# Two chunks of both up steps without the seven-product scheme, bias sums on another engine, and a new layout of the down step's tiles

## The chip, the cores and the metric

The kernel runs on one core of one Trainium2 chip, as one launch. The metric is the device time of a run in microseconds, the median of several runs. Engines are named as in the profile: PE (TensorE, matrix products), DVE (VectorE), ACT (ScalarE), POOL (GpSimd), SP (SyncE, which here mostly issues transfers).

## The reference, cut to what matters

Two transformer blocks in fp32, over 1024 tokens of width 1024. The parts that the change touches are the two feed-forwards, the biases of the second block's neighbourhood attention, and the norm at the start of the second block:

```python
# end of block 1, then the norm that ends it
u = rmsnorm(h, norm_mlp_g) @ w_up            # 1024 -> 4096
h = h + jnp.square(jax.nn.relu(u)) @ w_down  # 4096 -> 1024
x = rmsnorm(h, norm_final_g)
# block 2
h = rms_norm(x, ln1_g);  z = h @ w_in + b_in
...
bias = rpb[:, d_row[:, None, None, :, None], d_col[None, :, :, None, :]]
scores = jnp.where(valid[:, :, None, :], scores + bias[None], -1e30)
...
h2 = rms_norm(x, ln2_g)
x = x + jnp.square(jax.nn.relu(h2 @ w_ff1)) @ w_ff2
return rms_norm(x, lnf_g)
```

## The kernel before, in words

Every fp32 product is computed in three: each operand is split into a high part (the value rounded to the fast format, a copy on ACT, L130) and a low part (the rest, a subtraction on DVE or POOL, L131), and high by high, high by low and low by high are summed in PSUM. In the trace these two lines are those of all splits; which one a row belongs to is told by its tile: `w` are weights, `x` the normed tokens of an up step, `part` the operands of a down step.

A feed-forward is `ff_up`, then `ff_down`. It runs twice: after block 1's cross attention, and at the very end. `ff_up` goes over 16 chunks c of 256 hidden columns. In each chunk the product of tokens (two halves j of 512) and weights (two halves k of the 1024 inputs by two halves f of the chunk) is done as seven products of sums of quarter blocks in place of eight products of the blocks themselves: product i takes X[i], a sum of the quarter blocks of the tokens, and W[c][i], one of the weights. A product is 12 matmuls 128x128 by 128x512 (L967), so a chunk has 84. Products 1 and 2 take tokens of the first half alone (X1, X2, split in a block ahead of the loop), all others take sums with the second half. `second()` makes those: it norms the second half (`normed`, tiles xn, L903), transposes it on PE (L242, into tp and sc), forms t1 and t2 on DVE (L938, L939) and splits X5, X6, X7, X3 and X4. It stands behind four products of chunks 0 and 1. In chunks 0 and 1 the products come in pairs, (0,1), (1,1), (0,2), (1,2), (0,5), and so on; from chunk 2 on the order is (c,1), (c-1,4), (c,5), (c,6), (c,2), (c,3), (c,7). Product 1 is copied from PSUM by ACT (L973), 5, 6 and the results by DVE (L852), the squared relu is L981 on ACT with a DVE product, or L985 on DVE. Results, tiles t2k out of 12 buffers, are stored to DRAM (`hid_d`) by transfers that POOL issues (L987), four a chunk.

In the first `ff_up` there is side work: `bias_tables`. A table is written to DRAM (`rpb_d`), and in 12 steps of two 128x2x384 tiles (`bt`, two slots) it is loaded (L1219), the mask tile is added (L1225, POOL, two 128x384 per tile), and four stores put it to `bias_d` (L1226). All of its transfers are issued by POOL, in the same queue as the hidden values' stores. A step (`work[0]`) comes behind product 4 and the loads of the next (`work[1]`) behind product 3.

`ff_down` reads the hidden values back and does seven products of 16 steps, each step 12 matmuls by four PSUM banks (L1128). Its tiles are laid, by `layout("down")`, over those of the up step: `wpool` (left parts), `xpool` (streamed operands), `rpool` (right parts) and nine kept tiles. Where a pool lies on a tile of the up step, its first writer waits until that tile has been read: over a t2k tile that is the landing of its store, over a weight tile the last matmul that reads it.

`block2` starts with the last down product's sums, row tile by row tile (`finish`, L1284 the product with the norm's gain, L1299 and L1302 two squares on ACT with row sums), then xn (L1313), then `to_T`, the transposes. A scheduler sets the final order on every engine by priorities, `high_priority` and `issue_after`; each engine then runs its instructions in that order, and a waiting one holds those behind it.

## Time and profile before

| | us |
|---|---|
| median of three runs | 3135.36 (3133.58 to 3139.14) |
| the profiled execution | 3136.28 |
| its span | 3134.5 |
| PE busy in it | 2913.7 (93%) |
| DVE busy | 2203.8 (70%) |
| ACT busy | 1233.1 (39%) |
| POOL busy | 420.1 (13%) |

Terms and rows are read from the profiled execution. Times in rows of a timeline count from the start of its span. The first up step runs from 857.85 to about 1219.9, the first down step until 1535.4, block 2 begins there, the second up step at 2451.12 and the second down step at 2806.63.

### The profile page before, as it was taken

The numbers are of one execution on the slowest core, as the hardware profiler recorded it, in microseconds if no ns is written. First come the engines' busy times: TensorE is split into PE (matmuls) and PEld (weight loads), VectorE is DVE, ScalarE is ACT, GpSimd is POOL, SyncE is SP. The second block draws the span as 40 slices with busy tenths as digits, with TensorE's granted clock in tenths as the row PEclk, the third lists the DMA queues.
The fourth block names the chain that finished last, engine by engine and source line by source line (L and its number), as shares of the span: only waits on it lengthen the run. The fifth ranks groups of instructions, "written<-read, shape, count | busy, mean of one in ns | idle before, by whom it ended". The sixth has DMA issues, their size and how long they took to land.

```text
span 3134.5 us, 39994 instructions
## 1 busy us (share of the span) xinstructions
PE 2913.7 (93%) x14548; PEld 2441.5 (78%) x14548; DVE 2203.8 (70%) x3895; ACT 1233.1 (39%) x2276; POOL 420.1 (13%) x450
## 2 busy tenths in 40 slices
PE   7898899999969989999689999999999699989997
PEld 5798888788858867788567789898788588877786
DVE  6997777555677875997557787644345776749976
ACT  4122665332432222444456655444211522224444
POOL 3240110000002661000101222200000011100000
PEclk9998999999989999999889999999999899999999
DMA  3225573211114667652211323567842233356522
GB/s 123 63 86 167 181 216 93 67 48 61 68 65 156 202 211 285 221 169 78 89 58 60 125 86 107 172 194 235 281 129 74 74 112 114 108 207 246 195 88 81
DMA packets 252501, 422.86 MB, mean 135 GB/s; under 512 B 27893, under 2 KB 130832, under 8 KB 252304
## 3 DMA queue, kind: packets, MB, share of 16 engines
q1 hardware_dynamic: 214240, 305.86, 30.5%
q0 software_dynamic: 28832, 95.57, 8.9%
q10 hardware_dynamic: 9232, 18.88, 1.6%
q8 instruction: 115, 1.88, 0.2%
q14 instruction: 82, 0.67, 0.1%
HBM read 310.75 MB, written 111.69 MB: 135 GB/s over the span
## 4 chain that ended last, share of the span: by engine, by line
PE 62%; DVE 14%; issue 9%; DMA 7%; POOL 3%; ACT 3%; SPq 1%; DVEq 0%; ACTq 0%; POOLq 0%
PE mm L208 16%; PE fd L1128 14%; PE ff L967 8%; PE mm L179 5%; PE mm L180 5%; PE mm L181 5%; DVE acc L423 2%; PE pv L669 2%; PE tp L735 1%; PE pv L1589 1%; DMA bt<-rpb_d 1%; DVE keep L1015 1%; PE tp L242 1%; DVE part L131 1%; POOL w L131 1%
## 5 line engine op out<-in xcount | busy, mean ns | idle before, releaser
L967 PE MATMUL ff<-x,w 128*128 128x512 f32 x2688 | 632.9, 396 | 52.3 <-DVE w L131 23.3
L967 PEld LDWEIGHTS ff<-x,w 128*128 128x128 f32 x2688 | 511.2, 191 | 169.0 <-DVE w L131 24.1
L1128 PE MATMUL fd<-part,part 128*128 128x512 f32 x2688 | 622.9, 393 | 13.1 <-ACT part L130 9.3
L1128 PEld LDWEIGHTS fd<-part,part 128*128 128x128 f32 x2688 | 505.5, 189 | 130.4 <-DVE part L131 14.9
L208 PE MATMUL mm<-xh,w 128*128 128x512 f32 x1792 | 532.4, 394 | 0.5 <-ACT lruC L1461 0.3
L208 PEld LDWEIGHTS mm<-xh,w 128*128 128x128 f32 x1792 | 337.1, 189 | 69.2 <-ACT lruC L1461 1.6
L130 ACT ACTIVATE part<-keep 128x512 fp32r<-128x512 f32 x384 | 224.4, 624 | 288.1 <-PE fd L1128 265.7
L208 PE MATMUL mm<-xl,w 128*128 128x512 f32 x896 | 316.6, 393 | 0.0
L131 DVE TENSOR_TENSOR part<-keep,part 128x512 fp32r<-128x512 f32 x384 | 249.9, 682 | 52.4 <-ACT part L130 52.1
L130 ACT ACTIVATE w<-raw 128x1024 fp32r<-128x1024 f32 (+1 forms) x132 | 134.9, 1033 | 287.7 <-PE mm L180 115.7
L131 POOL TENSOR_TENSOR w<-raw,w 128x1024 fp32r<-128x1024 f32 x56 | 169.9, 3039 | 548.1 <-ACT w L130 523.2
L208 PEld LDWEIGHTS mm<-xl,w 128*128 128x128 f32 x896 | 169.3, 189 | 33.5
L852 DVE TENSOR_TENSOR t2k<-ff,t2k 128x512 f32<-128x512 f32 x160 | 109.7, 688 | 105.0 <-PE ff L967 94.3
L423 DVE SCALAR_TENSOR_TENSOR acc<-u,conv_wh,acc 128x1023 f32<-128x1023 f32 (+14 forms) x120 | 172.8, 1480 | 3.1 <-ACT acc L418 1.3
L234 DVE TENSOR_TENSOR h<-h,mm 128x512 f32<-128x512 f32 x176 | 119.5, 685 | 78.4 <-PE mm L181 77.7
L179 PE MATMUL mm<-w,xh 128*128 128x256 f32 x512 | 147.3, 288 | 15.3 <-DVE u L449 11.5
L130 ACT ACTIVATE w<-wr 128x512 fp32r<-128x512 f32 x160 | 97.4, 630 | 151.9 <-PE ff L967 62.3
L180 PE MATMUL mm<-w,xh 128*128 128x256 f32 x512 | 146.4, 286 | 0.0
L181 PE MATMUL mm<-w,xl 128*128 128x256 f32 x512 | 146.4, 286 | 0.0
L987 POOL DMA_DIRECT2D hid_d<-t2k x128 | 69.8, 546 | 494.9 <-DVE t2k L852 258.0
L131 DVE TENSOR_TENSOR w<-wr,w 128x512 fp32r<-128x512 f32 x160 | 112.3, 718 | 31.8 <-ACT w L130 30.4
L131 DVE TENSOR_TENSOR w<-raw,w 128x1024 fp32r<-128x1024 f32 (+1 forms) x76 | 89.1, 1178 | 44.9 <-ACT w L130 44.8
(350 smaller groups left out, 5076.1 us busy)
## 6 DMA issues: line engine op xcount, KB each, us to landing
hid_d<-t2k POOLq DMA_DIRECT2D x128, 256.0 KB, 2.9
x<-hid_d SPq DMA_DIRECT2D x128, 256.0 KB, 3.9
keep<-hid_d SPq DMA_DIRECT2D x96, 256.0 KB, 6.0
raw<-in_w_in_dram SPq DMA_DIRECT2D x40, 512.0 KB, 3.7
qk_d<-t2k SPq DMA_DIRECT2D x64, 256.0 KB, 2.6
wr<-in_w_up_dram SPq DMA_DIRECT2D x32, 512.0 KB, 3.7
keep<-in_w_down_dram SPq DMA_DIRECT2D x64, 256.0 KB, 4.8
wr<-in_w_ff_dram SPq DMA_DIRECT2D x32, 512.0 KB, 3.7
```

The source lines that it names most:

```text
L130: nc.scalar.activation(hi, src, AF.Copy)
L131: (eng or nc.vector).tensor_tensor(out=lo, in0=src, in1=fp(hi), op=ALU.subtract)
L179: nc.tensor.matmul(ps, sh, mh, start=(i == 0), stop=False)
L180: nc.tensor.matmul(ps, sh, ml, start=False, stop=False)
L181: self.last = nc.tensor.matmul(ps, sl, mh, start=False, stop=(i == n - 1))
L208: self.last = nc.tensor.matmul(pj[j], a, b, start=(k == 0 and q == 0), stop=(k == nk - 1 and q == 2))
L234: self.added[t] = self.nc.vector.tensor_tensor(out=hs, in0=hs, in1=ps, op=ALU.add)
L423: nc.vector.scalar_tensor_tensor(out=acc[m][:, lo:hi], in0=u[m][:, lo + d : hi + d], scalar=w(k), in1=acc[m][:, lo:hi], op0=ALU.mult, op1= ...
L852: tt = lambda o, x, y, op: nc.vector.tensor_tensor(out=o, in0=x, in1=y, op=op)
L967: b.last = nc.tensor.matmul(ps, l[:, k, :], r, start=(opens and k == 0 and q == 0), stop=(k == 3 and q == 2), skip_group_check=True)
L987: stored.append(nc.gpsimd.dma_start(out=hid[2 * c + f, :, j * 512 : (j + 1) * 512], in_=o))
L1128: last = nc.tensor.matmul(ps[q], l[:, sl], r, start=(c == 0 and x == 0), stop=(c == C - 1 and x == 2))
```

## The change

Chunks 0 and 1 of both up steps are computed by the eight products of the blocks themselves, 96 matmuls instead of 84 (`plain`): first both chunks for the first token half, then both for the second. `second()` now splits the second half as it is (`r12` and X3) and forms t1 and t2; a new `third()` makes X5, X6, X7 and X4 out of them behind the plain products. The side work begins behind the plain products: the table there, then a step behind product 2 and its loads behind product 3, both also behind that product's last DVE instruction. The sums of the bias tiles are DVE's. The first transposes of block 2 are tied to the last down product. In `layout("down")` the nine kept tiles come first, then right parts, streamed operands, left parts. The diff, cut to its core:

```diff
--- before.py
+++ after.py
@@ -63,13 +63,11 @@
         self.ff = ff
         if ff == "down":
 
-            self.kpool = [pool("ffd0", 1)]
-            self.keeps = [self.kpool[0].tile([P, 2, 512], F32, tag=f"k{q}", name=self.nm("keep")) for q in range(2)]
+            self.kpool = pool("ffd", 1)
+            self.keeps = [self.kpool.tile([P, 2, 512], F32, tag=f"k{q}", name=self.nm("keep")) for q in range(9)]
+            self.rpool = pool("ffr", 3)
+            self.xpool = pool("ffx", 8)
             self.wpool = pool("ffw", 3)
-            self.xpool = pool("ffx", 8)
-            self.rpool = pool("ffr", 3)
-            self.kpool.append(pool("ffd1", 1))
-            self.keeps += [self.kpool[1].tile([P, 2, 512], F32, tag=f"k{q}", name=self.nm("keep")) for q in range(2, 9)]
         elif ff:
 
             self.wk = pool("ffk", 12)
@@ -850,6 +848,9 @@
...
+    PLAIN = 2
 
     def weights(c):
 
@@ -862,12 +863,17 @@
...
+        def part(i, src, pool=None):
+            t = (pool or (b.wpool2 if i in (1, 2, 5) else b.wpool)).tile([P, 2, 4, P], F32R, tag="w", name=b.nm("w"))
             b.split(t[:, 0], t[:, 1], src)
             L[i] = t[:, 0], t[:, 1]
 
-        s1 = b.t2k((P, 4, P)) if c else b.slot(30, (P, 4, P), name="s")
+        if c < PLAIN:
+            for k in range(2):
+                for f in range(2):
+                    part((f, k), blk(f, k), (b.wpool2, b.wpool)[c])
+            return L
+        s1 = b.t2k((P, 4, P))
...
@@ -884,14 +890,19 @@
     W = {0: weights(0)}
 
 
...
+    tags = {
+        1: range(0, 4), 2: range(4, 8), 3: range(24, 28), 4: range(8, 12), 5: range(12, 16), 6: (28, 29, 30, 20),
+        7: range(16, 20), "r12": range(12, 16),
+    }
     X = {i: [None] * 4 for i in tags}
 
...
     def normed(t0):
         out = []
@@ -925,34 +936,63 @@
     def second():
         with b.tc.high_priority(offset=400):
             xn = normed(4)
-            pairs = [b.slot(21 + q, (P, 2, 512), name="t") for q in range(2)]
-            t1 = [pairs[k // 2][:, k % 2] for k in range(4)]
-            t23 = []
...
+                for n, i in enumerate(("r12", 3)):
+                    b.split(*xout(i, k), ps[n], scale=gs[n])
...
+        return t1, t2
+
+    def third(t1, t2):
+        with b.tc.high_priority(offset=200):
+
+            for k in range(4):
                 xpart(5, k, t1[k])
             for k in range(4):
-                xpart(6, k, t23[k][:, 0])
-
+                xpart(6, k, t2[k])
             for k in range(4):
-                tt(t1[k], t23[k][:, 0], r1[k][0], ALU.subtract)
+                tt(t1[k], t2[k], r1[k][0], ALU.subtract)
                 xpart(7, k, t1[k])
             for k in range(4):
-                tt(t1[k], r1[k][1], t23[k][:, 0], ALU.subtract)
+                tt(t2[k], r1[k][1], t2[k], ALU.subtract)
             for k in range(4):
-                xpart(3, k, t23[k][:, 1])
-            for k in range(4):
-                xpart(4, k, t1[k])
+                xpart(4, k, t2[k])
 
     banks, sums, stored = {}, {}, []
+
+    def send(c, f, j, o):
+        stored.append(nc.gpsimd.dma_start(out=hid[2 * c + f, :, j * 512 : (j + 1) * 512], in_=o))
+
+    def square(c, f, j, ps):
+        o = b.t2k()
+        nc.scalar.activation(o, ps, AF.Relu)
+        last = tt(o, o, o, ALU.mult)
+        send(c, f, j, o)
+        return last
+
+    def plain(c, j, ks, ps):
+
+        for k in ks:
+            x = X[((1, 2), ("r12", 3))[j][k]]
+            for f in range(2):
+                wh, wl = W[c][f, k]
+                for q in range(4):
+                    xh, xl = x[q]
+                    for n, (l, r) in enumerate(((wh, xh), (wh, xl), (wl, xh))):
+                        b.last = nc.tensor.matmul(
+                            ps[f], l[:, q, :], r, start=(k == 0 and q == 0 and n == 0), stop=(k == 1 and q == 3 and n == 2)
+                        )
+                if k == 1:
+                    with b.tc.high_priority(offset=400):
+                        square(c, f, j, ps[f])
 
...
     W[1] = weights(1)
-    order = [(c, i) for i in (1, 2, 5, 6, 7, 3) for c in (0, 1)] + [(0, 4)]
-    for c in range(2, 15):
+    pair = lambda: [b.ps2.tile([P, 512], F32, tag=t, name=b.nm("ff")) for t in ("mm", "pv")]
+    for c in range(PLAIN):
+        plain(c, 0, (0, 1), pair())
+    t1, t2 = second()
+    ps = [pair() for _ in range(PLAIN)]
+    for k in range(2):
+        for c in range(PLAIN):
+            plain(c, 1, (k,), ps[c])
+    third(t1, t2)
+    order = [(PLAIN, i) for i in (1, 2, 5, 6, 7, 3)]
+    for c in range(PLAIN + 1, 15):
         order += [(c, 1), (c - 1, 4)] + [(c, i) for i in (5, 6, 2, 3, 7)]
     order += [(15, 1), (14, 4), (15, 2)] + [(15, i) for i in (5, 6, 3, 7, 4)]
     work = None
-    for n, (c, i) in enumerate(order):
-        if n == 4:
-            second()
-        if i == 1 and 1 <= c < 15:
-            W[c + 1] = W.get(c + 1) or weights(c + 1)
-            work = side.popleft() if side else None
-        product(c, i)
-        if work and i in (4, 3):
-
-            with b.tc.issue_after(stored[-1].ins):
+    W[PLAIN] = weights(PLAIN)
+    if side:
+        with b.tc.issue_after(stored[-1].ins):
+            side.popleft()[1]()
+    for c, i in order:
+        if i == 1 and c < 15:
+            W[c + 1] = weights(c + 1)
+            if side:
+                work = side.popleft()
+        last = product(c, i)
+        if work and i in (2, 3):
+
+            with b.tc.issue_after(stored[-1].ins), b.tc.issue_after(last.ins):
                 work[i == 3]()
             if i == 3:
                 work = None
@@ -1110,7 +1161,7 @@
...
@@ -1222,7 +1273,7 @@
...
-            nc.gpsimd.tensor_tensor(out=t[:, x], in0=t[:, x], in1=m, op=ALU.add)
+            nc.vector.tensor_tensor(out=t[:, x], in0=t[:, x], in1=m, op=ALU.add)
             nc.gpsimd.dma_start(out=b.bias_d[head + x, n, :, half], in_=t[:, x])
 
     def step(k):
@@ -1316,7 +1367,8 @@
             ys.append(y)
         for g in (g0, g0 + 2):
             if g < 4:
-                b.to_T(ys[g : g + 2], g, b.g_ln1, xT)
+                with b.tc.issue_after(b.last.ins):
+                    b.to_T(ys[g : g + 2], g, b.g_ln1, xT)
             else:
                 b.bg.append((0, lambda ys=ys[g - 4 : g - 2], g=g: b.to_T(ys, g, b.g_ln1, xT, 100)))
     xT += b.halves(range(8, 16))
```

On PE, at the start of the first up step (ff is a chunk's PSUM tile, x a token operand, tp and sc the transposes' tiles, L242 before and L240 after), before:

```order
L967 MATMUL ff_8685<-x_8592,w_8504 128x512 x3
L967 MATMUL ff_8685<-x_8611,w_8504 128x512 x3
L967 MATMUL ff_8685<-x_8630,w_8504 128x512 x3
L967 MATMUL ff_8685<-x_8649,w_8504 128x512 x3
L242 MATMUL tp_8829<-ident,xn_8777 128x128
L242 MATMUL sc_8830<-ident,xn_8777 128x128
L242 MATMUL tp_8846<-ident,xn_8777 128x128
L242 MATMUL sc_8847<-ident,xn_8777 128x128
```

and after:

```order
L990 MATMUL ff_8658<-x_8578,w_8506 128x512 x3
L990 MATMUL ff_8658<-x_8597,w_8506 128x512 x3
L990 MATMUL ff_8658<-x_8616,w_8506 128x512 x3
L990 MATMUL ff_8658<-x_8635,w_8506 128x512 x2
L240 MATMUL tp_8828<-ident,xn_8773 128x128
L240 MATMUL sc_8829<-ident,xn_8773 128x128
L240 MATMUL tp_8846<-ident,xn_8773 128x128
L240 MATMUL sc_8847<-ident,xn_8773 128x128
L990 MATMUL ff_8658<-x_8635,w_8506 128x512
```

Before, transposes begin behind 12 matmuls of this list and 16 of them stand together; after, 23 plain matmuls precede the first and further plain ones stand between them.

On ACT, at the end of the first down step (w<-raw is a weight split of block 2's first projection, the L1299/L1302 and L1350/L1353 rows are the squares of the row tiles), before:

```order
L130 ACTIVATE part_13679<-keep_11243 128x512
L1299 ACTIVATE t2k_13799,sm_13797<-h_11260 128x1024
L1302 ACTIVATE t2k_13802,sm_13797<-h_11260 128x1024
L1299 ACTIVATE t2k_13804,sm_13797<-h_11261 128x1024
L130 ACTIVATE w_14043<-raw_14041 128x1024
L130 ACTIVATE w_14049<-raw_14047 128x1024
L1302 ACTIVATE t2k_13807,sm_13797<-h_11261 128x1024
L1299 ACTIVATE t2k_13809,sm_13797<-h_11262 128x1024
L130 ACTIVATE w_14203<-raw_14201 128x1024
L1302 ACTIVATE t2k_13812,sm_13797<-h_11262 128x1024
```

and after:

```order
L1350 ACTIVATE t2k_13788,sm_13786<-h_11250 128x1024
L1353 ACTIVATE t2k_13791,sm_13786<-h_11250 128x1024
L1350 ACTIVATE t2k_13793,sm_13786<-h_11251 128x1024
L1353 ACTIVATE t2k_13796,sm_13786<-h_11251 128x1024
L1350 ACTIVATE t2k_13798,sm_13786<-h_11252 128x1024
L128 ACTIVATE w_14032<-raw_14030 128x1024
L128 ACTIVATE w_14038<-raw_14036 128x1024
L1353 ACTIVATE t2k_13801,sm_13786<-h_11252 128x1024
L1350 ACTIVATE t2k_13803,sm_13786<-h_11253 128x1024
L128 ACTIVATE w_14192<-raw_14190 128x1024
```

The square L1302 of the second row tile moved from behind two weight splits to a place ahead of them, with the first square of the third.

The sums of the bias tiles, before on POOL (L987 stores a hidden tile, L1219 loads, L1225 sums, L1226 stores a bias tile):

```order
L987 DMA hid_d_8497<-t2k_9930 128x512
L1219 DMA bt_9398<-rpb_d 128x2x384
L1225 TENSOR_TENSOR bt_9396<-bt_9396,pr_9243 128x384 x2
L1226 DMA bias_d<-bt_9396 128x384 x2
L1215 DMA pr_9851<-in_c_maskN_dram 128x384
L1225 TENSOR_TENSOR bt_9398<-bt_9398,pr_9243 128x384 x2
L1226 DMA bias_d<-bt_9398 128x384 x2
L1219 DMA bt_9549<-rpb_d 128x2x384
L987 DMA hid_d_8497<-t2k_9984 128x512
```

and after on DVE (L850 with ff evacuates a product, L129 splits a weight, L851 squares):

```order
L850 TENSOR_TENSOR t2k_10074<-ff_9942,t2k_9909 128x512
L851 SCALAR_TENSOR_TENSOR t2k_10074<-t2k_10074 128x512
L1276 TENSOR_TENSOR bt_9693<-bt_9693,pr_9540 128x384 x2
L850 TENSOR_TENSOR t2k_10091<-ff_10078,t2k_10060 128x512
L1276 TENSOR_TENSOR bt_9695<-bt_9695,pr_9540 128x384 x2
L129 TENSOR_TENSOR w_10029<-t2k_10021,w_10029 128x512
L850 TENSOR_TENSOR t2k_10021<-t2k_10021,wr_10017 128x512
L850 TENSOR_TENSOR t2k_10106<-ff_10093,t2k_10060 128x512
L850 TENSOR_TENSOR wr_10018<-wr_10018,t2k_10021 128x4x128
L129 TENSOR_TENSOR w_10034<-t2k_10021,w_10034 128x512
```

The sums left POOL's queue, where they stood among loads and stores, and stand among DVE's evacuations and weight splits.

## Rows read from the trace of the kernel before

**Rows 1.** The page, the costliest groups: busy, mean ns | idle before, releaser.

```profile
L967 PE MATMUL ff<-x,w 128*128 128x512 f32 x2688 | 632.9, 396 | 52.3 <-DVE w L131 23.3
```

**Rows 2.** TensorE's waits, 855 to 1225: us, times, longest.

```profile
PE ff L967 <- DVE t2k L852: 13.8, 9, 6.3
PE ff L967 <- DVE w L131: 11.6, 1, 11.6
PE tp L242 <- DVE xn L903: 6.4, 2, 4.3
PE ff L967 <- ACT t2k L973: 6.1, 1, 6.1
PE fd L1128 <- DVE part L131: 3.1, 2, 1.9
```

**Rows 3.** TensorE's waits, 2449 to 2836.

```profile
PE fd L1128 <- ACT part L130: 9.3, 1, 9.3
...
PE ff L967 <- DVE t2k L852: 0.8, 1, 0.8
```

**Rows 4.** TensorE's timeline, first up step's start: start, us, instruction, [idle before].

```profile
857.85 2.44 PE L967 MATMUL ff<-x,w 128*128 128x512 f32 x10
...
912.62 2.93 PE L967 MATMUL ff<-x,w 128*128 128x512 f32 x6 [6.13 <-ACT t2k L973]
```

**Rows 5.** TensorE's timeline, second up step's start.

```profile
2451.12 0.40 PE L967 MATMUL ff<-x,w 128*128 128x512 f32 x1
...
2489.09 12.42 PE L967 MATMUL ff<-x,w 128*128 128x512 f32 x46 [11.62 <-DVE w L131]
2507.70 4.64 PE L967 MATMUL ff<-x,w 128*128 128x512 f32 x10 [6.19 <-ACT t2k L973]
```

**Rows 6.** Windows: stretch, busy us (instructions), granted clock, DMA share.

```profile
857.00:913.00 56.00, 31.30 (x122) 0.75 0.16 57
2508.00:2797.00 289.00, 288.22 (x1260) 0.99 0.34 117
```

**Rows 7.** VectorE's timeline, first up step's start.

```profile
887.59 4.90 DVE L131 TENSOR_TENSOR x<-t,x 128x512 fp32r<-128x512 f32 x8
892.41 1.29 DVE L131 TENSOR_TENSOR w<-wr,w 128x512 fp32r<-128x512 f32 x2
```

**Rows 8.** The bias tiles: min/median/max ns; POOL's idle time by end; landing.

```profile
L1225 POOL TENSOR_TENSOR bt<-bt,pr x48: 997/1022/1466, 1022.7 to 1190.4; 128x384 f32<-128x384 f32 x48
...
  DMA bt<-rpb_d: 15.7, 10
  DMA bias_d<-bt: 11.6, 7
...
DMA to landing us min/median/max: 2.2/3.3/6.8
```

**Rows 9.** VectorE's groups by line, 1022 to 1200: busy, mean ns | idle before.

```profile
L852 DVE TENSOR_TENSOR t2k<-ff,t2k 128x512 f32<-128x512 f32 x42 | 28.8, 685 | 15.3 <-DMA hid_d<-t2k 8.2 <-PE ff L967 6.9
...
L131 DVE TENSOR_TENSOR w<-t2k,w 128x512 fp32r<-128x512 f32 x16 | 19.2, 1202 | 0.1
L852 DVE TENSOR_TENSOR t2k<-t2k,wr 128x512 f32<-128x512 f32 x8 | 14.4, 1799 | 0.3
```

**Rows 10.** VectorE's groups by line, 2620 to 2797.

```profile
L131 DVE TENSOR_TENSOR w<-t2k,w 128x512 fp32r<-128x512 f32 x16 | 11.1, 693 | 0.2
...
L852 DVE TENSOR_TENSOR t2k<-t2k,wr 128x512 f32<-128x512 f32 x8 | 5.5, 692 | 0.3
```

**Rows 11.** ScalarE's timeline, start of the second down step.

```profile
2805.95 1.67 ACT L130 ACTIVATE part<-x 128x512 fp32r<-128x512 f32 x3 [11.81 <-DMA hid_d<-t2k]
```

**Rows 12.** TensorE's and ScalarE's timeline, start of block 2.

```profile
1558.73 1.35 PE L242 MATMUL sc<-ident,xn 128*128 128x128 f32 x4 [23.35 <-DVE xn L1313]
...
1534.73 2.00 ACT L130 ACTIVATE w<-raw 128x1024 fp32r<-128x1024 f32 x2 [9.96 <-PE fd L1128]
...
1546.35 1.06 ACT L1302 ACTIVATE t2k<-h 128x1024 bf16<-128x1024 f32 x1 [0.52 <-DVE h L1284]
```

More of the change, by code (lines that the diff above doesn't have):

```diff
@@ L852, in ff_up @@
     tt = lambda o, x, y, op: nc.vector.tensor_tensor(out=o, in0=x, in1=y, op=op)
+    stt = lambda o, x, c, y, p0, p1: nc.vector.scalar_tensor_tensor(out=o, in0=x, scalar=c, in1=y, op0=p0, op1=p1)
+    PLAIN = 2
     def weights(c):
@@ L863, in weights @@
         L = {}
-        def part(i, src):
-            t = (b.wpool2 if i in (1, 2, 5) else b.wpool).tile([P, 2, 4, P], F32R, tag="w", name=b.nm("w"))
+        def part(i, src, pool=None):
+            t = (pool or (b.wpool2 if i in (1, 2, 5) else b.wpool)).tile([P, 2, 4, P], F32R, tag="w", name=b.nm("w"))
             b.split(t[:, 0], t[:, 1], src)
             L[i] = t[:, 0], t[:, 1]
-        s1 = b.t2k((P, 4, P)) if c else b.slot(30, (P, 4, P), name="s")
+        if c < PLAIN:
[4 more added lines that the diff above has]
+        s1 = b.t2k((P, 4, P))
         part(1, blk(0, 0))
@@ L884, in ff_up, with xout @@
     W = {0: weights(0)}
-    r2at = (28, 29, 30, 20)
-    tags = {1: range(0, 4), 2: range(4, 8), 3: range(8, 12), 5: range(12, 16), 6: range(24, 28), 7: range(16, 20), 4: r2at}
+    tags = {
+        1: range(0, 4), 2: range(4, 8), 3: range(24, 28), 4: range(8, 12), 5: range(12, 16), 6: (28, 29, 30, 20),
+        7: range(16, 20), "r12": range(12, 16),
+    }
     X = {i: [None] * 4 for i in tags}
+    def xout(i, k):
+        t = b.slot(tags[i][k], (P, 2, 512), F32R, "x")
+        X[i][k] = t[:, 0], t[:, 1]
+        return X[i][k]
     def xpart(i, k, src):
-        t = b.slot(tags[i][k], (P, 2, 512), F32R, "x")
-        b.split(t[:, 0], t[:, 1], src)
-        X[i][k] = t[:, 0], t[:, 1]
+        b.split(*xout(i, k), src)
     def normed(t0):
@@ L927, in second @@
             xn = normed(4)
-            pairs = [b.slot(21 + q, (P, 2, 512), name="t") for q in range(2)]
-            t1 = [pairs[k // 2][:, k % 2] for k in range(4)]
-            t23 = []
+            pair = lambda q: b.slot(q, (P, 2, 512), name="t")
+            t1 = [t[:, q] for t in (pair(21), pair(22)) for q in range(2)]
+            t23 = pair(23)
+            t2 = [t23[:, 0], t23[:, 1], b.t2k(), b.t2k()]
             for k in range(4):
@@ L941, in second @@
+                stt(t1[k], ps[0], gs[0], r1[k][0], ALU.mult, ALU.subtract)
+                stt(t2[k], ps[1], gs[1], t1[k], ALU.mult, ALU.subtract)
+        return t1, t2
+    def third(t1, t2):
+        with b.tc.high_priority(offset=200):
+            for k in range(4):
                 xpart(5, k, t1[k])
             for k in range(4):
-                xpart(6, k, t23[k][:, 0])
+                xpart(6, k, t2[k])
             for k in range(4):
-                tt(t1[k], t23[k][:, 0], r1[k][0], ALU.subtract)
+                tt(t1[k], t2[k], r1[k][0], ALU.subtract)
@@ L978, in product @@
                 return
+            f, j = {2: (0, 0), 3: (0, 1), 7: (1, 1), 4: (1, 0)}[i]
+            if i == 2:
+                return square(c, f, j, ps)
             o = b.t2k()
-            if i == 2:
-                nc.scalar.activation(o, ps, AF.Relu)
-                tt(o, o, o, ALU.mult)
-            else:
-                tt(o, ps, sums[c, {3: 6, 7: 5, 4: 1}[i]], ALU.add)
-                nc.vector.scalar_tensor_tensor(out=o, in0=o, scalar=0.0, in1=o, op0=ALU.max, op1=ALU.mult)
-            f, j = {2: (0, 0), 3: (0, 1), 7: (1, 1), 4: (1, 0)}[i]
-            stored.append(nc.gpsimd.dma_start(out=hid[2 * c + f, :, j * 512 : (j + 1) * 512], in_=o))
-    W[1] = weights(1)
-    order = [(c, i) for i in (1, 2, 5, 6, 7, 3) for c in (0, 1)] + [(0, 4)]
-    for c in range(2, 15):
+            tt(o, ps, sums[c, {3: 6, 7: 5, 4: 1}[i]], ALU.add)
+            last = stt(o, o, 0.0, o, ALU.max, ALU.mult)
+            send(c, f, j, o)
+            return last
+    W[1] = weights(1)
+    pair = lambda: [b.ps2.tile([P, 512], F32, tag=t, name=b.nm("ff")) for t in ("mm", "pv")]
[9 more added lines that the diff above has]
+    for c in range(PLAIN + 1, 15):
         order += [(c, 1), (c - 1, 4)] + [(c, i) for i in (5, 6, 2, 3, 7)]
@@ L1112, in ff_down @@
                 last_parts += [
-                    b.kpool[q > 1].tile([P, 2, 512], F32R, tag=f"k{q}", name=b.nm("part")) for q in (0, 1, 8)
+                    b.kpool.tile([P, 2, 512], F32R, tag=f"k{q}", name=b.nm("part")) for q in (0, 1, 8)
                 ]
```

5 lines of the change are left out of this document (removed).

## The prediction, as it was put down before the changed kernel ran

> **What bounds the kernel now.** I read the page first. The costliest group of the whole kernel is TensorE's (PE's) up matmul: 2688 instructions, 632.9 us busy, and 52.3 us of idle time in front of them [rows 1]. So work on another engine counts here only through TensorE: its idle time, its slow clock, and the number of its matmuls. Next come the waits of TensorE in the two feed-forwards, to see who ends its idle time [rows 2, 3]. In the first (up step, then the start of the down step) VectorE results t2k cost 13.8 us in 9 waits, a weight split w 11.6, the normed rows xn 6.4, a ScalarE copy 6.1, and a part of the down step 3.1. In the second t2k falls to 0.8, the down step's part costs 9.3, and the wait on w returns to the tenth (11.62, [rows 5]). Three places follow: the starts of both up steps, the middle of the first alone, and the ends of both. The timeline gives the places in time [rows 4, 5], the windows give the clock and the rate [rows 6]. VectorE's own timeline says why the start waits [rows 7]; its groups, with the bias tile's, why the middle does [rows 8 to 10]; ScalarE's timeline the down step [rows 11] and the boundary [rows 12].
>
> The rate: 1260 matmuls in 288.22 busy us at a clock of 0.99, so 0.229 us each [rows 6]; seven products of 12 are 19.2 us.
>
> **Start of the up steps.** Until 912.62 the first up step has run 84 up matmuls and 32 transposes since 857.85, in 54.8 us; the second needs 56.6 (2451.12 to 2507.70) for the same and 8 transposes more (by my count in the timeline, whose ends stand in [rows 4, 5]). 84 matmuls are 19.2 us, the transposes about 3.4 and 4.3 at half a pitch (an estimate: 128 columns against 512). So 32.2 and 33.1 us are lost: 24.1 of the first in waits on w, xn and the copy [rows 2], the other 8 in work at a granted clock of 0.75 in the mean of this stretch [rows 6]. The cause is in [rows 7]: VectorE works without a pause on splits of the second token half (8 in 4.90, so 0.61 us from one to the next), and only at 892.41 reaches the split w on which TensorE stands for 11.6 us [rows 2].
>
> The change puts 96 matmuls (22 us) that need only the first half and four weight splits per chunk in front, where before 48 did; the other 96 need the second half but just its two plain splits. Sums for X5, X6, X7 and X4 move under those. VectorE's whole demand from 857.85 to the third chunk's part 5: before, it got to w at 892.4 after 34.5 us; added are 4 splits (8 plain splits instead of four copies on ScalarE and four splits), 8 squares at 0.69, and some 6 us of weight splits, 49 us in sum. TensorE asks for that part after 96 + 96 + 24 matmuls, 49.5 us, and 32 transposes, 3.4: 53 us. Supply and demand are thus nearly level, and no wait of 11.6 or 6.1 should remain. What is late next is the normed rows: the transposes still stand 23 matmuls into the step, 5.3 us, against the 6.4 us lost on xn now, and small waits on weights. I estimate 7.5 us lost per start: half of the xn waits (3.2), a few waits for the chunks' weights (2 to 3), 2 us at the low clock. From below 3 us (xn alone), from above 19.5 (one of the 11.6 us waits comes back).
> The plain chunks cost 12 matmuls more each, 24 per up step: 5.5 us at 0.229, all on TensorE, so on the path. Gain: 32.2 - 7.5 - 5.5 = 19.2 and 33.1 - 7.5 - 5.5 = 20.1, together 39.3; between 15 and 48 with the bounds.
>
> **Bias sums.** The 48 adds take 1.02 us each on POOL, from 1022.7 to 1190.4, which is 14 us for each of 12 groups of four [rows 8]. Two things speak for their share in the 13.8 us. First, while they run VectorE is slow: a w<-t2k split takes 1202 ns against 693 in the same place of the second up step, a t2k<-t2k,wr 1799 against 692: 17 us in these two groups alone (16 x 0.51 + 8 x 1.11) [rows 9, 10]. Second, POOL's queue also issues the hidden stores, and stands behind bias transfers: 15.7 us for loads and 11.6 for stores [rows 8], and the 42 evacuations of VectorE stand 8.2 us behind hid_d<-t2k [rows 9], which is a t2k buffer not free. The adds on VectorE, about 0.5 us each (a 128x512 takes 0.69), cost 25 us of its time, most of which the lengthening gives back: it has room. But now VectorE, in order, stands behind the loads too. In the new order the adds of tiles 0 to 13, seven groups of two, stand among 13 evacuations, 50 us of TensorE's work at five per 19.2 us; a round trip is 9 by the medians (load 3.3 us to land, two adds, two issues, stores 3.3 to land [rows 8]), and 12 by POOL's pace (14, less 4 adds shorter by 0.5); I take 10.5. Six intervals are 63 us against 50, so 13 us at first and about 10 after what TensorE's PSUM banks and t2k tiles buffer; later groups have a whole chunk, 19.2 us, for one trip and stand free. So 13.8 becomes about 10, less the 0.8 that the last product shows in both up steps: a gain of 3. Ends: nothing remains (gain 13), or 6 x 12 - 50 = 22, of which the buffers take 2 (loss 7).
> The Trainium skill ("SBUF — State Buffer", Who interferes with whom) has a rule that a VectorE instruction with two SBUF inputs contends with a GpSimd instruction that reads SBUF. The trace agrees: 1202 ns against 693, while evacuations, which read one operand from PSUM, stay at 685 [rows 9]. By that rule alone the whole middle would come free; the sum goes by the in-order wait above.
>
> **Down steps.** The left parts' pool lay on tiles that hold hidden values until their stores land: ScalarE idles 11.81 us <-DMA hid_d<-t2k before its first part of the second down step [rows 11], TensorE 9.3 behind it [rows 3]; in the first down step 3.1 in two waits on parts [rows 2]. The new layout lays kept tiles there, which are loads, and the left parts over chunk 15's weights, which product 3 before the last has done with; the right part waits for the last but two instead of the last. So 2.8 of 3.1 and 9 of 9.3 should go. What is late next is the DMA: the kept tiles now wait for those stores. They are needed only some steps later (a step is 12 matmuls, 2.7 us). I take off 1 us: gain 11; ends 0 and 12.
>
> **Block 2.** TensorE's order at this boundary is the same in both: transposes already stood behind the last down product. ScalarE's is not: a weight split w<-raw that waits for TensorE's end, 9.96 us until 1534.73, stood in front of the second square L1302 of row tile 1; it runs 2 us later, and tile 3's only at 1546.35 [rows 12], while TensorE stands 23.35 us for xn. In the new order that square and the next L1299 come before the wait, so tiles 1 and 2 lead. One (2 us) or two (4) squares' steps leave the chain of tiles: 4, with 2 and 6 as ends (nothing if the last down sums' own time rules).
>
> **Sum**, against the profiled execution of 3136.28 us (span 3134.5, and 1.8 around it): -39.3 - 3 - 11 - 4 = -57, that is 3079; its time stands 0.9 over the median of 3135.36; I say 3080, rounded up.
>
> **Rivals.**
> A, slower: VectorE's in-order queue stands for a full round trip in every group, not in the first six intervals only. There are 12 groups; 12 x 10.5 = 126 against the 13 now, +113, and with -54 of the other parts 3195. For it: in all of POOL's issues the next load stands behind the last group's stores, as in [rows 8]. Against it: later groups have 19.2 us for a trip of 10.5. It decides from a stand of 6 us per group, (57 + 13)/12.
> B: the middle is port contention alone, all 13 us go: 3069. For it the 1202 ns; against, VectorE's own waits on hid_d.
> C: VectorE bounds the start again, an 11.6 us wait returns in front of part 5 of the third chunk in each start, less the 3 of weights already counted: +17, 3096. For it: 49 us of demand against 53 of supply, a margin of 4.
> D: the down step is bound by its loads, which start behind the stores: the 11 are given back, 3090.
> E: the boundary's order does nothing: 3083, inside the forecast.
>
> **Chances.** Forecast 0.60 (3068 to 3092 with E), B 0.10, C 0.15, D 0.07, A 0.05, others on the slow side 0.03. Range 3058 to 3106: it holds the forecast, B, C and D, and leaves A. Under 0.2% (6.3 us) nothing can be told from no change: faster 0.92, same 0.02, slower 0.06.
>
> **What would show it.** At both up starts the idle time in front of the first plain matmuls and of part 5 of the third chunk under 8 us in all, none of 11.6; the clock of that stretch above 0.9. In the middle DVE idle behind bt<-rpb_d of 1 to 5 us each, in the first half only, and w<-t2k near 693 ns. ScalarE's wait before the first part of the second down step under 2 us. The first transpose of block 2 about 19 us after the last down matmul. A single DVE wait on bt in every chunk would make A right; a wait of 6 us or more on w in the starts would make C right; idle TensorE on DMA loads after the first 16 down steps, D.

## The result, and the profile after

The changed kernel takes 3052.53 us (median of three runs, 3051.61 to 3057.36) against 3135.36: the ratio is 0.9738 with an interval of 0.9716 to 0.9760. The profiled execution took 3052.53 us with a span of 3050.8, 83.7 less than before. The forecast was 3080 with a range down to 3058: the direction was right, and the measured time lies 5.5 us below the range.

Stage by stage (us): the stages are bounded by the first up matmul, the first down matmul, the end of the last down matmul and the first matmul of block 2's projection, in the two timelines of TensorE.

| stage | before | after | difference |
|---|---|---|---|
| ahead of the first up step | 857.9 | 859.2 | +1.3 |
| first up step | 361.9 | 328.6 | -33.2 |
| first down step | 315.7 | 307.0 | -8.6 |
| start of block 2 | 45.6 | 38.9 | -6.7 |
| block 2 to its up step | 870.2 | 870.2 | 0.0 |
| second up step, with the wait behind it | 355.5 | 322.8 | -32.7 |
| second down step | 311.0 | 307.1 | -3.9 |
| end | 16.9 | 16.9 | 0.0 |

TensorE's waits after, first up step and the start of its down step (us in total, times, longest), against [rows 2]:

```profile
PE ff L1007 <- DVE t2k L850: 4.7, 3, 3.7
PE ff L1007 <- ACT w L128: 3.8, 2, 2.7
PE fd L1179 <- DVE part L129: 0.5, 1, 0.5
PE tp L240 <- DVE xn L914: 0.3, 1, 0.3
```

The wait on t2k fell from 13.8 us to 4.7, the 11.6 on w and the copy's 6.1 are gone (3.8 on ScalarE's w is new), xn fell from 6.4 to 0.3, and the down step's part from 3.1 to 0.5. The same for the second feed-forward, against [rows 3]: of the wait of 9.3 for a part, 0.5 remains.

```profile
PE ff L1007 <- ACT w L128: 3.5, 2, 2.5
PE ff L1007 <- DVE t2k L850: 0.8, 1, 0.8
PE fd L1179 <- DVE part L129: 0.5, 1, 0.5
```

TensorE's timeline at the start of the first up step (start, us, instruction, idle time before), against [rows 4]:

```profile
859.19 5.38 PE L990 MATMUL ff<-x,w 128*128 128x512 f32 x23
864.90 0.30 PE L240 MATMUL tp<-ident,xn 128*128 128x128 f32 x1 [0.34 <-DVE xn L914]
...
911.14 6.00 PE L1007 MATMUL ff<-x,w 128*128 128x512 f32 x24 [1.06 <-ACT w L128]
919.88 5.47 PE L1007 MATMUL ff<-x,w 128*128 128x512 f32 x17 [2.74 <-ACT w L128]
```

From 859.19 to 919.88 are 60.7 us, in which TensorE runs the 192 plain matmuls, 36 of chunk 2 and the 32 transposes. At the 0.229 us of [rows 6] and the transposes' 3.4 that is 55.6 us of work, so 5.1 are lost where 32.2 were. The window has the clock at full, 1.00 where [rows 6] shows 0.75:

```profile
857.00:913.00 56.00, 54.60 (x254) 1.00 0.21 76
```

ScalarE's first part of the second down step no longer waits 11.81 us ([rows 11]); it waits 2.72 for a load, 11 us ahead of TensorE's first down matmul:

```profile
2715.61 0.63 ACT L128 ACTIVATE part<-x 128x512 fp32r<-128x512 f32 x1 [2.72 <-DMA x<-hid_d]
```

At the end of the first down step and the start of block 2 (TensorE, against [rows 12]) the wait on xn is 16.70 us where it was 23.35:

```profile
1187.84 1.07 PE L1179 MATMUL fd<-part,part 128*128 128x512 f32 x4
1189.39 305.50 PE L1179 MATMUL fd<-part,part 128*128 128x512 f32 x1340 [0.48 <-DVE part L129]
1511.58 1.35 PE L240 MATMUL sc<-ident,xn 128*128 128x128 f32 x4 [16.70 <-DVE xn L1364]
...
1533.81 1.65 PE L206 MATMUL mm<-xh,w 128*128 128x512 f32 x3 [0.19 <-ACT xh L131]
```

On ScalarE the second square of row tile 1 runs at 1485.57, ahead of the wait for TensorE's end. That of tile 3 runs at 1502.22, 8 us behind the first weight split (1494.24), where before it was 11.6 us behind it (1534.73):

```profile
1485.57 1.06 ACT L1353 ACTIVATE t2k<-h 128x1024 bf16<-128x1024 f32 x1 [1.29 <-DVE h L1335]
...
1494.24 2.00 ACT L128 ACTIVATE w<-raw 128x1024 fp32r<-128x1024 f32 x2 [6.48 <-PE fd L1179]
...
1502.22 1.04 ACT L1353 ACTIVATE t2k<-h 128x1024 bf16<-128x1024 f32 x1
```

VectorE's groups in the middle of the first up step (busy, mean ns, idle before), against [rows 9, 10]: the lengthening is gone, and the bias sums stand 4.4 us behind their loads.

```profile
L850 DVE TENSOR_TENSOR t2k<-ff,t2k 128x512 f32<-128x512 f32 x48 | 32.9, 685 | 15.8 <-PE ff L1007 15.6
...
L1276 DVE TENSOR_TENSOR bt<-bt,pr 128x384 f32<-128x384 f32 x48 | 24.4, 553 | 6.5 <-DMA bt<-rpb_d 4.4 <-issue 2.1
...
L129 DVE TENSOR_TENSOR w<-t2k,w 128x512 fp32r<-128x512 f32 x18 | 12.4, 689 | 0.1
...
L850 DVE TENSOR_TENSOR t2k<-t2k,wr 128x512 f32<-128x512 f32 x9 | 6.2, 693 | 0.3
```

### The profile page after: what moved, and what is told of

It reads as the page before. It is cut to its first block, busy times and chain, and to the rows that moved or that the text cites. A ratio compares the mean times of both kernels' runs of the same rounds, so it can differ in the third digit from the quotient of the medians.

```text
span 3050.8 us, 40049 instructions
## 1 busy us (share of the span) xinstructions
PE 2900.2 (95%) x14596; PEld 2440.8 (80%) x14596; DVE 2162.9 (71%) x3903; ACT 1231.9 (40%) x2272; POOL 369.5 (12%) x402
## 4 chain that ended last, share of the span: by engine, by line
PE 79%; DVE 10%; DMA 4%; ACT 3%; issue 2%; POOL 1%; SPq 0%; DVEq 0%; ACTq 0%; POOLq 0%
PE fd L1179 20%; PE mm L206 18%; PE ff L1007 15%; PE mm L177 5%; PE mm L179 5%; PE mm L178 5%; DVE acc L421 2%; PE ff L990 2%; PE pv L667 2%; PE tp L733 2%; PE pv L1641 1%; PE tp L240 1%; POOL w L129 1%; DMA bt<-rpb_d 1%; ACT w L128 1%
## 5 line engine op out<-in xcount | busy, mean ns | idle before, releaser
L1179 PE MATMUL fd<-part,part 128*128 128x512 f32 x2688 | 613.2, 390 | 1.0 <-DVE part L129 1.0
L1007 PE MATMUL ff<-x,w 128*128 128x512 f32 x2352 | 541.6, 392 | 13.0 <-ACT w L128 7.3
L1007 PEld LDWEIGHTS ff<-x,w 128*128 128x128 f32 x2352 | 443.7, 189 | 110.6 <-ACT w L128 9.0
L129 DVE TENSOR_TENSOR part<-keep,part 128x512 fp32r<-128x512 f32 x384 | 249.2, 683 | 47.2 <-ACT part L128 47.0
L128 ACT ACTIVATE w<-raw 128x1024 fp32r<-128x1024 f32 (+1 forms) x132 | 134.9, 1033 | 282.6 <-PE mm L178 111.5
L129 POOL TENSOR_TENSOR w<-raw,w 128x1024 fp32r<-128x1024 f32 x56 | 170.9, 3056 | 493.7 <-ACT w L128 491.2
L850 DVE TENSOR_TENSOR t2k<-ff,t2k 128x512 f32<-128x512 f32 x140 | 96.3, 688 | 82.1 <-PE ff L1007 80.8
L129 DVE TENSOR_TENSOR w<-raw,w 128x1024 fp32r<-128x1024 f32 (+1 forms) x76 | 89.2, 1179 | 47.1 <-ACT w L128 47.0
L129 DVE TENSOR_TENSOR w<-wr,w 128x512 fp32r<-128x512 f32 x156 | 104.4, 686 | 15.8 <-ACT w L128 14.0
```

The source lines that it names most:

```text
L128: nc.scalar.activation(hi, src, AF.Copy)
L129: (eng or nc.vector).tensor_tensor(out=lo, in0=src, in1=fp(hi), op=ALU.subtract)
L850: tt = lambda o, x, y, op: nc.vector.tensor_tensor(out=o, in0=x, in1=y, op=op)
L1007: b.last = nc.tensor.matmul(ps, l[:, k, :], r, start=(opens and k == 0 and q == 0), stop=(k == 3 and q == 2), skip_group_check=True)
L1179: last = nc.tensor.matmul(ps[q], l[:, sl], r, start=(c == 0 and x == 0), stop=(c == C - 1 and x == 2))
```

## The experiments

Each ran beside the kernel before on the same chip, and its ratio is to that kernel; so two variants from different chips are compared by their ratios. "The changed kernel" stands at 0.9738. Times of stages come from one profiled execution of each variant; the first up step took 328.6 us in the changed kernel and 332.0 in the run with the old layout, which has the same up step, so 3 us between two such figures can be scatter. Code cuts in the edits are marked with dots.

**The layout of the down step undone**

```diff
-            self.kpool = pool("ffd", 1)
...
+            self.kpool = [pool("ffd0", 1)]
...
+            self.wpool = pool("ffw", 3)
+            self.xpool = pool("ffx", 8)
             self.rpool = pool("ffr", 3)
-            self.xpool = pool("ffx", 8)
-            self.wpool = pool("ffw", 3)
+            self.kpool.append(pool("ffd1", 1))
...
```

> The changed kernel with the down step's tiles laid as before. Theory: the layout alone ends the waits at both starts of the down step (3.4 and 9.3 us before), the stretch at the low clock behind them (about 5 and 4 us), and, since ScalarE's order at the start of block 2 is again the old one, 6.7 us there: 28 us slower than the changed kernel, about 3081, with the clock near 0.5 in the 5 us behind the first down step's waits. Rival: the layout is worth its waits only, 11 to 13 us, and the start of block 2 belongs to the tie of the transposes: about 3065.

Measured 3082.16, ratio 0.9827 (0.9803 to 0.9851), 0.9% slower than the changed kernel.

**The layout alone in the kernel before**

```diff
-            self.kpool = [pool("ffd0", 1)]
...
+            self.kpool = pool("ffd", 1)
...
+            self.rpool = pool("ffr", 3)
+            self.xpool = pool("ffx", 8)
             self.wpool = pool("ffw", 3)
-            self.xpool = pool("ffx", 8)
-            self.rpool = pool("ffr", 3)
...
```

> The kernel before with the new layout of the down step alone. Theory: 28 us faster than before (12.7 of waits, 9 of low clock behind them, 6.7 at the start of block 2): about 3107. Rival (only the waits at the down steps' starts, as forecast): 11 us, about 3124.

Measured 3108.10, ratio 0.9908 (0.9883 to 0.9933). Both runs agree with 28 us for the layout. The kernel before with the new layout has down steps of 307.1 and 307.1 us and a start of block 2 of 38.8; the changed kernel with the old layout has 314.4, 310.9 and 45.7. So the start of block 2 belongs to the layout too: with the old one ScalarE's order there is the old one. The tie of the transposes moves nothing that these runs show: the first kernel has no tie and the short start, 38.8 against the 38.9 of the changed kernel, and the second has the tie and the long start, 45.7 against the 45.6 of the kernel before.

**Matmuls that nobody reads in the wait ahead of the down step**, with the old layout

```diff
...
+    for q in range(14 if first else 42):
+        with b.tc.issue_after(b.last.ins):
+            b.last = nc.tensor.matmul(fill, W[15][1][0][:, 0, :], X[4][3][0], start=True, stop=True)
```

> The changed kernel with the old layout, and behind the last up product 14 (first up step) and 42 (second) matmuls 128x128 by 128x512 whose result nobody reads, so that TensorE works through most of the wait at the start of the down step. Clock theory: the stretch at the low clock behind the waits goes, 5 us in the first down step and 4 in the second, less about 1 where the added matmuls outlast a wait: 7 to 9 us faster than the old layout without them, about 3073. Rival: the slow stretch is the loads' doing (DMA share above 1.0 there) and no clock effect, so nothing is won: 3081 or slower.

Measured 3080.66, ratio 0.9827 (0.9811 to 0.9843): the same as without them. The clock did what was expected. The window of TensorE behind the wait (busy, instructions, granted clock, DMA share, GB/s) is, with the old layout and then with the added matmuls:

```profile
1192.00:1197.00 5.00, 5.00 (x17) 0.68 1.04 398
```

```profile
1192.00:1197.00 5.00, 4.63 (x22) 1.00 1.03 383
```

At the same DMA share of 1.03 the five microseconds hold 22 matmuls instead of 17, so the slow stretch is the clock's and not the loads'. But it is worth about 1 us in each feed-forward and not 4 to 5: up step and down step together take 645.0 us with the added matmuls and 646.4 without, in the second feed-forward 640.4 and 641.4. The rest of what the old layout's down step loses is lost later. The weight loads of TensorE (PEld) that waited, old layout:

```profile
1191.06 72.66 PEld L1181 LDWEIGHTS fd<-part,part 128*128 128x128 f32 x314 [2.22 <-DVE part L131]
1263.89 2.60 PEld L1181 LDWEIGHTS fd<-part,part 128*128 128x128 f32 x12 [0.17 <-DVE part L131]
...
1305.98 2.59 PEld L1181 LDWEIGHTS fd<-part,part 128*128 128x128 f32 x12 [0.41 <-DVE part L131]
```

From 1263.89 to 1305.98 the steps follow each other in 3.01 us on average, where 12 matmuls take 2.72. There VectorE has five instructions per step, two splits, two sums and a result of the product before, and they take those 3.0 us:

```profile
1298.64 1.27 DVE L131 TENSOR_TENSOR part<-keep,part 128x512 fp32r<-128x512 f32 x2
1299.85 1.27 DVE L1068 TENSOR_TENSOR keep<-x,keep 128x512 f32<-128x512 f32 x2
1301.05 0.67 DVE L1068 TENSOR_TENSOR h<-h,fd 128x512 f32<-128x512 f32 x1
1301.65 1.27 DVE L131 TENSOR_TENSOR part<-keep,part 128x512 fp32r<-128x512 f32 x2
```

In the changed kernel VectorE is ahead, so TensorE runs through until 1290.34, and only five steps wait for a part instead of fourteen:

```profile
1189.39 100.55 PEld L1179 LDWEIGHTS fd<-part,part 128*128 128x128 f32 x444 [0.90 <-DVE part L129]
1290.34 2.61 PEld L1179 LDWEIGHTS fd<-part,part 128*128 128x128 f32 x12 [0.40 <-DVE part L129]
...
1302.36 27.76 PEld L1179 LDWEIGHTS fd<-part,part 128*128 128x128 f32 x123 [0.42 <-DVE part L129]
```

That lead is from the start of the step: in the first 41 us VectorE was busy for 25.27 us with the old layout and for 31.39 with the new one (old, then new).

```profile
1191.00:1232.00 41.00, 25.27 (x42) 0.96 1.04 392
```

```profile
1191.00:1232.00 41.00, 31.39 (x51) 1.00 1.04 392
```

The kernel before shows the same late steps, from 1300.76 to 1342.85:

```profile
1300.76 2.60 PEld L1128 LDWEIGHTS fd<-part,part 128*128 128x128 f32 x12 [0.41 <-DVE part L131]
...
1342.85 157.19 PEld L1128 LDWEIGHTS fd<-part,part 128*128 128x128 f32 x694 [0.39 <-DVE part L131]
```

The second down step repeats it: before, such rows run from 2879.99 to 2925.08, fifteen steps of 3.01 us; after, from 2829.31 to 2841.33, four.

**The bias sums back on GpSimd**

```diff
-            nc.vector.tensor_tensor(out=t[:, x], in0=t[:, x], in1=m, op=ALU.add)
+            nc.gpsimd.tensor_tensor(out=t[:, x], in0=t[:, x], in1=m, op=ALU.add)
```

> The changed kernel with the bias sums back on GpSimd. Theory: the middle of the first up step loses 9 us of TensorE's waits and about 2 at a low clock again: about 3064, VectorE's w<-t2k near 1200 ns there. Rival: the new place of the side work, not the engine of the sums, is what freed the middle: within 3 us of 3052.5.

Measured 3067.52, ratio 0.9776 (0.9751 to 0.9801): the theory holds and the rival does not. In its profiled execution, the slowest of its four (3076.19), the first up step takes 343.2 us instead of 328.6 and TensorE waits 14.1 us on t2k again. VectorE's w<-t2k is slow again, 1033 ns; the group t2k<-t2k,wr, 1799 ns in the kernel before, stays at 692:

```profile
PE ff L1007 <- DVE t2k L850: 14.1, 9, 4.3
```

```profile
L129 DVE TENSOR_TENSOR w<-t2k,w 128x512 fp32r<-128x512 f32 x16 | 16.5, 1033 | 0.1
...
L850 DVE TENSOR_TENSOR t2k<-t2k,wr 128x512 f32<-128x512 f32 x8 | 5.5, 692 | 0.3
```

**The sums on VectorE in the kernel before, nothing else**

```diff
-            nc.gpsimd.tensor_tensor(out=t[:, x], in0=t[:, x], in1=m, op=ALU.add)
+            nc.vector.tensor_tensor(out=t[:, x], in0=t[:, x], in1=m, op=ALU.add)
```

> The kernel before with its bias sums on VectorE and nothing else changed; the side work stands at its old places. Theory (GpSimd's reads make VectorE late, and that costs the middle): 11 to 15 us faster than before, 3120 to 3124. Rival (as forecast): VectorE then stands behind the loads for about 10 us, so only 3 us come back, 3132; a part of the gain would then belong to the new places of the side work.

Measured 3132.99, ratio 0.9997 (0.9983 to 1.0011): no change in the time, as the rival had it. In the profiled execution the first up step is 3.0 us shorter (358.8 against 361.9), so that much the sums alone may win. VectorE stands 17.0 us behind the loads, where the side work is at its old places, and 4.4 us at the new ones. VectorE's wait in this run, then the bias tile's in the changed kernel:

```profile
DVE bt L1225 <- DMA bt<-rpb_d: 17.0, 9, 4.7
```

```profile
  DMA bt<-rpb_d: 4.4, 6
```

**GpSimd reads, writes, and writes for as long**, sums kept on VectorE

```diff
...
+            for y in range(2):
+                nc.gpsimd.tensor_tensor(out=junk, in0=m[:, y * 192 : y * 192 + 192], in1=m[:, y * 192 : y * 192 + 192], op=ALU.add)
```

> The changed kernel with two sums 128x192 of the mask tile on GpSimd ahead of each bias store, into a tile that nobody reads; the bias sums stay on VectorE. GpSimd reads SBUF some 50 us more. Contention theory: VectorE's instructions with two SBUF inputs become longer again (w<-t2k toward 1000 ns and more) and TensorE's waits in the middle of the first up step return in good part: 5 to 12 us slower than the changed kernel, 3058 to 3065. Queue theory (it was GpSimd's queue that was late with loads and hidden stores): slower too, by the same as the variant that only writes.

Measured 3064.13, ratio 0.9776 (0.9759 to 0.9792). Next, memsets in the same places:

```diff
...
+            for _ in range(2):
+                nc.gpsimd.memset(junk, 0.0)
```

> The same with two memsets 128x192 in the same places of GpSimd's queue, which write SBUF and read nothing. Contention theory: VectorE's instructions keep 690 ns and the middle stays free, within 3 us of the changed kernel, at most 3056. Queue theory: as slow as the variant that reads, 3058 to 3065.

Measured 3057.76, ratio 0.9755 (0.9737 to 0.9773), just above the 3056 of the contention theory. A memset turned out half as long as the sum (275 against 594 ns), so this alone does not part the theories, and the memsets were doubled:

```diff
...
+            for _ in range(4):
+                nc.gpsimd.memset(junk, 0.0)
```

> Four memsets 128x192 ahead of each bias store, twice the two of before (275 ns each), so that GpSimd is held as long as by the two sums of the reading variant (594 ns each), and reads nothing. Contention theory: as the variant with two memsets, 3055 to 3059, VectorE's instructions stay at 690 ns. Queue theory (GpSimd's time, not its reads): as the reading variant, 3062 to 3067.

Measured 3057.01, ratio 0.9750 (0.9733 to 0.9766). The reading variant, TensorE's wait on t2k, VectorE's groups and then GpSimd's added instructions (`fill` is the tile that nobody reads):

```profile
PE ff L1007 <- DVE t2k L850: 15.8, 6, 6.4
```

```profile
L1279 DVE TENSOR_TENSOR bt<-bt,pr 128x384 f32<-128x384 f32 x48 | 34.6, 765 | 8.6 <-DMA bt<-rpb_d 8.3 <-issue 0.3
...
L129 DVE TENSOR_TENSOR w<-t2k,w 128x512 fp32r<-128x512 f32 x18 | 13.5, 748 | 0.1
```

```profile
L1281 POOL TENSOR_TENSOR fill<-pr 128x192 f32<-128x192 f32 x96 | 57.0, 594 | 2.9
```

and that with four memsets:

```profile
PE ff L1007 <- DVE t2k L850: 8.6, 4, 4.0
```

```profile
L1279 DVE TENSOR_TENSOR bt<-bt,pr 128x384 f32<-128x384 f32 x48 | 24.3, 554 | 13.3 <-DMA bt<-rpb_d 13.3
...
L129 DVE TENSOR_TENSOR w<-t2k,w 128x512 fp32r<-128x512 f32 x18 | 12.4, 690 | 0.1
```

```profile
L1281 POOL MEMSET fill<- 128x192 f32 x192 | 51.6, 269 | 5.6
```

GpSimd is held about as long (57.0 and 51.6 us), but only its reads lengthen VectorE's instructions (765 against 554 ns, 748 against 690). The first up step is 342.5 us with the reads, 334.5 with four memsets, 330.5 with two, 328.6 with nothing added. So of the 13.9 us that the reading variant adds there, 8 are the reads', and up to 6 are GpSimd's time in its queue (VectorE then waits 13.3 us for the loads). The ratios bear this out less sharply: those with memsets do not part from the changed kernel's, and the intervals of the reading variant and of four memsets just overlap. The Trainium skill ("SBUF — State Buffer", Who interferes with whom) states just this split, that VectorE with two SBUF inputs contends with a GpSimd instruction that reads SBUF and not with one that only writes it; these two traces agree.

**One plain chunk**

```diff
-    PLAIN = 2
+    PLAIN = 1
```

> The changed kernel with one plain chunk instead of two. Theory (supply against VectorE's demand): 96 + 24 matmuls and the transposes give 31 us until the next chunk's part 5, VectorE needs about 46, so 15 us of waits and some 5 at a low clock come back in each start, less 2.7 for 12 matmuls saved and the 4 us of waits there now: about +27, 3080. Rival: it is only the missing order of the splits that cost the time, and one chunk does as well: 5 us faster by 24 matmuls, 3047.

Measured 3100.18, ratio 0.9883 (0.9859 to 0.9906), 20 us more than expected. This form splits chunk 1's weights twice, since two lines ask for them, and TensorE waits 21.6 us at once on a weight split. With that split done once:

```diff
-    PLAIN = 2
+    PLAIN = 1
...
-    W[PLAIN] = weights(PLAIN)
+    W[PLAIN] = W.get(PLAIN) or weights(PLAIN)
```

> One plain chunk, with the split of chunk 1's weights done once (the first form did it twice). Theory (supply against VectorE's demand): in the first form VectorE reaches the next chunk's first split 38 us behind the first up matmul, and TensorE has run out after 27, so about 12 us of waits per start, some 3 at a low clock, less 2.7 of matmuls saved and the 4 us of waits that the changed kernel has: +8 per start, 3069. Rival: nothing but the doubled split cost the 47 us, so it is at 3047 (24 matmuls saved).

Measured 3071.95, ratio 0.9807 (0.9784 to 0.9829), near the 3069 of the theory. One wait of the old size is back in each up step, in the first one 39 us behind its start, on VectorE's split:

```profile
894.13 11.35 PE L1007 MATMUL ff<-x,w 128*128 128x512 f32 x39 [11.34 <-DVE w L129]
```

**Two attempts at a better one**

```diff
             for k in range(4):
                 xpart(6, k, t2[k])
+            W[PLAIN] = weights(PLAIN)
...
-    W[PLAIN] = weights(PLAIN)
```

> The changed kernel with chunk 2's weight splits asked for ahead of the sums for X7 and X4. The order of VectorE moves by a few instructions only: theory, the waits on w in front of part 5 of chunk 2 (1.06 us in each up step) go and the next ones shrink by as much: 3 us faster at most, 3049 to 3052.5. Rival: TensorE's wait just moves to another part: no change.

Measured 3054.06, ratio 0.9742 (0.9728 to 0.9757): no change. TensorE's two waits on ScalarE's w, 3.8 us in the first up step, became one of 3.2.

```diff
-        return self.wk.tile(list(shape), dt, tag="t2k", name=self.nm("t2k"), bufs=12 if self.ff else 4)
+        return self.wk.tile(list(shape), dt, tag="t2k", name=self.nm("t2k"), bufs=10 if self.ff else 4)
...
-        raw = [b.rpool.tile([P, 4, 256], F32, tag="raw", name=b.nm("wr")) for _ in range(2)]
+        raw = []
+        for k in range(2):
+            q = (2 * c + k) % 3
+            raw.append((b.wk if q == 2 else b.rpool).tile([P, 4, 256], F32, tag=f"raw{q}", name=b.nm("wr"), bufs=1))
```

> The changed kernel with three buffers for the raw weights of the up steps instead of two, the third in the place of two of the 12 t2k buffers. Theory: the waits of 2.7, 3.7 and 2.5 us that stand on a load of raw weights (VectorE and ScalarE wait for wr<-in_w_up) go, 6 to 9 us faster: 3044 to 3047. Rival: ten t2k buffers are too few while the bias transfers hold GpSimd's queue, so TensorE waits on t2k instead: 3053 or slower.

Measured 3050.17, ratio 0.9727 (0.9712 to 0.9741): faster than the kernel before, but its interval does not part it from the changed kernel's. Its up steps are 327.0 and 319.7 us against 328.6 and 322.8; TensorE's waits in the first up step are 8.8 us as they were 8.5, on other tiles.

## Why the prediction was wrong

The forecast added up 57 us and 83.7 were measured. Of the 27 us between them 20 lie in two terms. **The step that failed is the pricing of the down steps**: "gain 11; ends 0 and 12" counts the waits at their starts and puts what stands behind these waits at nothing. Measured are 22.8 us. The second is the bias sums, 3 forecast and 11.6 measured, within the ends that were given (a gain of 13, a loss of 7).

**Starts of the up steps: right.** 39.3 us were forecast. The first lost 32.2 and now loses 5.1, at 5.5 more matmul time: a gain of 21.6. The second runs from 2403.97 to the end of its last wait on w at 2465.62, 61.65 us, of which 52.1 are matmuls and 4.3 transposes: it lost 33.1 and now loses 5.2, a gain of 22.4. Together 44, inside the bounds; the wait on xn that I kept at 3.2 is 0.3, and the clock stayed at 1.00 in the window of the first. The balance of VectorE's demand and TensorE's supply holds: with half the supply the wait is back at 11.3 us.

**Down steps: a term left out.** "2.8 of 3.1 and 9 of 9.3 should go": 2.6 and 8.8 went, so the waits were priced rightly. The first down step fell by 8.6 us, the second by 3.9, and the second up step's stage by 10.3 more than its start gained (32.7 less 22.4): 22.8 in all. What was left out is the late steps. Where the late VectorE is the bound of a later product, at 3.01 us per step against 2.72, the late start is paid a second time 75 to 120 us on: nine or ten more steps at 0.29 us, nearly 3 us in each down step. The low clock adds 1 to 2 us in the first, as the windows of the kernel before show, 13 matmuls in 5 us where 22 run at full clock:

```profile
1224.00:1229.00 5.00, 5.00 (x13) 0.50 1.03 395
1229.00:1234.00 5.00, 5.00 (x22) 0.92 1.04 391
```

With about 1 us of low clock in the second (what the added matmuls won there), waits, late steps and clock make 19 to 20 of the 22.8 us; the rest is about as large as the scatter of an up step and stays open. The 12 us that I took as the most counted neither the late steps nor the clock.

**Bias sums: the term was mis-sized, by the time that VectorE stands behind the loads.** "So 13.8 becomes about 10", a gain of 3. What is left of the first up step's 33.2 us beside its start is 11.6. The trip of a group, from one group's stores to the next's, is 9.1 us (the first stores of two groups are issued at 1008.1 and 1017.2 in POOL's timeline), the medians' 9 and not the 10.5 that I took toward POOL's old pace. And six intervals do not add up to one wait: the loads land while VectorE has other work, so it stands 4.4 us in all and not the 13 of the forecast. What the forecast priced came about in another kernel, the one before with the sums on VectorE: it stands 17.0 us and its time does not change. The new places alone were not run in the kernel before; with the sums on GpSimd the changed kernel's up step takes 343.2 us, 18.7 less than before, which is less than its start gained. So neither of the two wins more than 3 us by itself, and both together 11.6. Rival B, the contention alone, had nearly this size, 13, but not the cause alone: taking GpSimd's reads away at the old places changed nothing. It named one half rightly: GpSimd's reads cost the up step 8 us more (342.5 against 334.5) than writes that hold GpSimd about as long.

**Block 2: right in the order, too small.** ScalarE's order was the lever, 6.7 us instead of 4, above the upper end of 6; it comes from the layout and not from the tie of the transposes. A part of the size is a collision that the forecast did not see: in the wait for xn VectorE stands behind GpSimd's weight splits. After the change two of its small instructions last until such a split ends, at 1504.7 and 1507.1:

```profile
1502.23 2.53 DVE L248 TENSOR_TENSOR sm<-sm,sm 128x4 f32<-128x4 f32 x2
1504.80 2.32 DVE L258 SCALAR_TENSOR_TENSOR sm<-sm,sm 128x4 f32<-128x4 f32 x1
1507.14 0.36 DVE L248 TENSOR_TENSOR sm<-sm,sm 128x4 f32<-128x4 f32 x2
```

```profile
1502.39 4.70 POOL L129 TENSOR_TENSOR w<-raw,w 128x1024 fp32r<-128x1024 f32 x2 [2.36 <-ACT w L128]
```

The first row takes 2.53 us where the third, of the same form, takes 0.36. The kernel before has three such stands (at 1546.24, 1550.57 and 1553.46, 2.2 to 2.5 us each), the changed one two, so about 2 of the 6.7 us are one collision fewer, and 4.3 us of the remaining 16.70 are collisions still. This is read from the traces; no run moved these splits.

**Rivals and signs.** A, C and D did not occur, nor did E: the boundary's order was worth 6.7 us. Of the signs two came out otherwise: ScalarE's wait before the first part of the second down step was 2.72 us and not under 2, which cost nothing, and the first transpose of block 2 stands 16.7 us behind the last down matmul and not 19.

**The sum.** 44 + 11.6 + 22.8 + 6.7 less 1.3 ahead of the first up step are 83.8, and 83.7 were measured; the terms are the stages regrouped, so this checks the reckoning and not the causes. All four terms came out larger than forecast; the two that count are the down steps by 12 us and the bias sums by 9.

## What to carry to other kernels

Price a wait at the start of a stage not by its length alone: look for the later place of the stage where the engine that starts late is the bound, and count the steps that it is late there. Where in-order queues share work, the position of an instruction and the engine that runs it belong to one term: here neither alone won more than 3 us, and both together 11.6. Before giving a part of a change a gain, take that part out and compare the order of each engine: here the tie of the transposes moved nothing, and the layout, which seemed to be about the down steps, moved ScalarE's order in block 2.
